# Sample attention of a hybrid decoder: 30 page buffers, operand pairs split two half-steps ahead, and a residual chunk loaded later

## The chip, the cores and the metric

The kernel runs on one core of a Trainium2 chip. The metric is the device time of one execution in microseconds (us). The engines are named as the profile names them: PE is TensorE (PEld its weight loads), DVE is VectorE, ACT is ScalarE, POOL is GpSimd, SP is SyncE, which issues every transfer here.

## What is computed

One inference step of two layers for a prompt of 1024 tokens and for 64 sample tokens (8 sequences of 8). The change is in the attention of the samples, which runs over 2048 cached positions for each sequence, in 16 pages of 128 rows that a table points to:

```
def one(args):
    qn_b, qr_b, c_b, kr_b, pt_b = args
    c_all = concat([ckv_pool[layer, pt_b].reshape(n_past, KV_RANK), c_b])       # 16 pages of 128 x 256
    kr_all = concat([krope_pool[layer, pt_b].reshape(n_past, QK_ROPE_DIM), kr_b])
    k_nope = rms_norm(einsum('bkc,chd->bkhd', c_all, w_uk), g_k_nope)
    s = (q_nope . k_nope + q_rope . kr_all) * SOFTMAX_SCALE
    p = softmax(where(mask, s, -inf))
    lat = einsum('bhqk,bkc->bqhc', p, c_all)          # the cached rows again, now as values
    return einsum('bqhc,chv->bqhv', lat, w_uv)
```

Then attention and pooling outputs go through one output projection, the residual `x` is added, and an MLP follows. All is float32: a matmul operand is split into a high and a low part, and three products stand for one.

## The kernel before, in words

`sample_attention` goes through 8 sequences (called batches, `b`) of 16 pages. One half-step `q` (0 to 15) handles one page of batch `b`: `keys(b, q)` multiplies the transposed page with `w_uk` and the queries (12 matmuls into the banks `pk`), ACT squares the result (`psq`, L990) and copies the scores (L991), and DVE sums the squares by head (`pss`, L992; there is exactly one such instruction to a half-step, so its start times mark the half-steps). At each even `q` the loop also issues the loads of two later pages (`load`, L870 and L871) and transposes the pair after next (`transp`: PE `cpt` L957, ACT `ch` L960, DVE `cl` L961): at step `q` the pages `q+2` and `q+3`.

In the same half-steps the previous batch's softmax and value product run (`slot(b - 1, q)`): exponentials at steps 6 and 7 (`weigh`, ACT L1048 and L1049), their low parts on DVE (`weigh_low`, L1054), and from step 8 to 15 the product of the weights with two cached pages a step (`latent`, PE L1074 and L1075). For that product a page is split once more, this time untransposed: `vsplit` makes the high part `vh` on ACT (L1060) and the low part `vl` on POOL (L1062; partly on DVE in the last batch). `vsplit` is the last reader of a page, so it frees the page's buffer `cp`. There are 26 such buffers; a new page takes the one that came free first.

`norm8(b)` at step 8 takes the reciprocal root of the first 8 pages' sums: two short instructions on DVE (L130, L138) and then 12 on POOL (L141 to L144); `scale8` at step 10 uses it. The order on PE, DVE, ACT and POOL in the loop is that in which the code is written (`manual_schedule`); SP's order is the scheduler's. Each engine works its list in order.

Behind the loop the last batch is drained (`slot` alone), and around this drain `fill` brings in the residual: `residual_load` reads 128 rows of `x` into one of three buffers `raw`, `residual` transposes them on PE (L1246) and ACT copies them into the residual `y` (L1247), which is kept in three chunks of columns (384, 384 and 320 tokens). `mix_load` reads the other inputs of the projection, and `op.chunk(group, c)` is the projection of chunk `c`, whose result DVE adds to `y[c]` (L315). After the drain `w_uv` is read (L1181), its product `so` computed (L1185), and the next weights (`w_out`, L94) are read through the same three buffers.

Of the kernel before, what the change touches and what calls it, by code (L numbers as in the profile page):

```python
# [10 lines left out]
F32 = mybir.dt.float32  # L11
F32R = mybir.dt.float32r
# [8 lines left out]
P = 128  # L21
D = 1024
KB = 8
# [5 lines left out]
CH = [(0, 384), (384, 768), (768, 1088)]  # L29
NTB = 9  # L30
# [5 lines left out]
R = 256  # L36
# [21 lines left out]
def pool(g, name, bufs=1, space=None, side=None):  # L58
    kw = {}
    if space is not None:  # L60
        kw["space"] = space
    if side is not None:
        kw["side"] = side
    if space is not DRAM:
        kw["reuse_waits"] = "tile"
    return g.tc.tile_pool(name=name, bufs=bufs, **kw)
# [771 lines left out]
def sample_attention(g, I, S, ahead, fill_start, fill):  # L838
    nc = g.nc
    SQ = H * DT  # L840
    with ExitStack() as st:
        sa = st.enter_context(pool(g, "sa", 2, side="right"))
# [16 lines left out]
        def load(b, pr):  # L859

            if pr % 2 == 0:
                kps[b, pr // 2] = sk.tile([P, 4, QR], F32, name="kp", tag="kp", bufs=3)
            kp = kps[b, pr // 2]
            for j in range(2):
                pg = pr * 2 + j
                n = b * NPG + pg
                with g.tc.issue_after(dmas[n - 8]) if n >= 8 else nullcontext():
                    v = nc.sync.value_load(ptb[0:1, n:n + 1], min_val=0, max_val=npool - 1)
                cp = sa.tile([P, R], F32, name="cp", tag="cp", bufs=26)
                nc.sync.dma_start(cp, I["cache_ckv"][0, ds(v, 1)].rearrange("o p c -> p (o c)"))  # L870
                di = nc.sync.dma_start(kp[:, (pr % 2) * 2 + j], I["cache_krope"][0, ds(v, 1)].rearrange("o p c -> p (o c)"))  # L871
                dmas.append(di.ins)
                cps[b, pg] = cp
# [44 lines left out]
        fold = sa.tile([P, 2, NS], F32, name="fold", bufs=1)  # L918
        nc.gpsimd.tensor_copy(fold, i2[:, None, :].to_broadcast([P, 2, NS]))

        VT = [(sa.tile([P, R + 2], F32R, name=f"vh{i}", bufs=1), sa.tile([P, R], F32R, name=f"vl{i}", bufs=1)) for i in range(4)]
        for vh, _ in VT:
            nc.gpsimd.memset(vh[:, R:].bitcast(F32), 1.0)
        latT = sa.tile([P, 2, H, NS], F32, name="latT", bufs=1)
# [71 lines left out]
        def norm8(b):  # L996
            ss = ss8[b].rearrange("p a h -> p (a h)")
            r = prs[b] = g.tiny.tile([P, 64], F32, name="prs", tag="prs", bufs=2)
            rsqrt(g, r, ss, 1.0 / QN, 64, eng=nc.gpsimd)

        def scale8(b, g8):
            r = prs.pop(b)
            s8 = sc[b][:, g8 * 8:g8 * 8 + 8]
            sv = s8.rearrange("p a (h t) -> p (a h) t", t=DT)
            nc.vector.tensor_tensor(sv, sv, r.unsqueeze(2).to_broadcast([P, 64, DT]), ALU.mult)
            sf = s8.rearrange("p a q -> p (a q)")
            nc.vector.tensor_tensor(sf, sf, pr8[b].rearrange("p a q -> p (a q)"), ALU.add)
# [8 lines left out]
        def soft1(b):  # L1016
            s = sc[b]
            nc.gpsimd.memset(s[NS:, NPG], NEG)
            nc.gpsimd.tensor_copy(s[:NS, NPG], snew[:NS, b].rearrange("p h t -> p (h t)"))
            mx = mxs[b]  # L1020
            nc.vector.tensor_reduce(mx[:, 1], s[:, 8:].rearrange("p a q -> p q a"), AX.X, ALU.max)
            nc.vector.tensor_tensor(mx[:, 0], mx[:, 0], mx[:, 1], ALU.max)

        def soft2(b):
            pt = msc("mxt")
            nc.tensor.transpose(pt[:SQ, :P], mxs.pop(b)[:, 0], g.ident)
            m1 = g.tiny.tile([P, 1], F32, name="m1", tag="m1", bufs=2)
            nc.vector.tensor_reduce(m1[:SQ], pt[:SQ, :P], AX.X, ALU.max)
            dg = sa.tile([P, SQ], F32, name="sdg", tag="sdg")
            nc.vector.tensor_scalar_mul(dg[:SQ], g.ident[:SQ, :SQ], m1[:SQ])  # L1030
            return dg
# [3 lines left out]
        def soft3(b, dg):  # L1035
            pb = mxb[b] = msc("mxb")
            nc.tensor.matmul(pb[:, :SQ], g.ones[:SQ], dg[:SQ], start=True, stop=True)
            ph_[b] = sa.tile([P, NPG + 1, 2, SQ], F32R, name="ph", tag="ph", bufs=1)
# [17 lines left out]
        vs = {}  # L1056

        def vsplit(b, pg):
            ch, c_l = vs[b, pg] = VT[pg % 4]
            nc.scalar.copy(ch[:, :R], cps[b, pg])  # L1060
            e = nc.vector if b == DB - 1 and pg % 4 else nc.gpsimd
            e.tensor_tensor(c_l, cps.pop((b, pg)), ch[:, :R].bitcast(F32), ALU.subtract)  # L1062
# [41 lines left out]
        def slot(b, q):  # L1104

            if not 0 <= b < DB:
                return
            if q == 0:
                norm8(b)
            elif q == 2:  # L1110
                scale8(b, 1)
            elif q == 3:
                soft1(b)
            elif q == 5:
                st_[b] = soft2(b)
            elif q == 6:
                soft3(b, st_.pop(b))
                shift(b, 0)
                weigh(b, 0)
                shift(b, 1)  # L1120
            elif q == 7:
                weigh_low(b, 0)
                weigh(b, 1)
            elif q == 8:
                weigh_low(b, 1)
            elif q == 16:
                latent(b, NPG)
                lat2(b)
            elif q == 17:
                lat3(b)  # L1130
            elif q == 20:
                lat4(b)
            if 8 <= q <= 15:
                for pg in (2 * q - 16, 2 * q - 15):
                    latent(b, pg)
            if 7 <= q <= 14:
                for pg in (2 * q - 14, 2 * q - 13):
                    vsplit(b, pg)

        begin(0)  # L1140
# [4 lines left out]
        with g.tc.manual_schedule(engines={ET.PE, ET.DVE, ET.Activation, ET.Pool}):  # L1145
            for n in range(2 * NJ):
                b, q = divmod(n, 16)
# [78 lines left out]
def residual_load(g, I, xts, tb):  # L1226
    nc = g.nc
    p = tbp(tb)
    xts[tb] = xt = raw_tile(g)[:, :1024]
    if tb < 8:  # L1230
        nc.sync.dma_start(xt, I["x_prompt"][0, tb * P:(tb + 1) * P, :])
    else:
        nc.sync.dma_start(xt[:p], I["x_sample"].rearrange("b t d -> (b t) d"))


def residual(g, y, xts, tb):

    nc = g.nc
    p = tbp(tb)
    c, off = tb // 3, (tb % 3) * P  # L1240
    xt = xts.pop(tb)
    for hf in range(2):
        pt = bank(g, "up", "xtp2").rearrange("p (a b) -> p a b", b=P)
        for k in range(4):
            kk = hf * 4 + k
            nc.tensor.transpose(pt[:, k, :p], xt[:p, kk * P:(kk + 1) * P], g.ident[:p, :p])  # L1246
        nc.scalar.copy(y[c][:, hf * 4:hf * 4 + 4, off:off + p], pt[:, :, :p])  # L1247
# [237 lines left out]
def step(ctx, tc, I, O):  # L1485
    nc = tc.nc
    g = G()
# [15 lines left out]
    g.ring = {"A": (g.wr, 2)}  # L1503
    constants(g, I)

    def ytiles(p):
        return [p.tile([P, KB, b - a], F32, name=f"y{c}", tag=f"y{c}", bufs=1) for c, (a, b) in enumerate(CH)]


    ya = ctx.enter_context(ExitStack())  # L1510
    g.lo = nc.gpsimd
    with ExitStack() as l0:
        l0p = l0.enter_context(pool(g, "l0", side="right"))
        S.q_s = l0p.tile([P, H, QH], F32, name="q_s")
        S.k_s = l0p.tile([P, H, QH], F32, name="k_s")
        S.kr = l0p.tile([P, NTB, QR], F32, name="kr")
        S.cs_h = l0p.tile([P, R + 2], F32R, name="cs_h")
        S.cs_l = l0p.tile([P, R], F32R, name="cs_l")
        with ExitStack() as a:
            wb = a.enter_context(pool(g, "wb0"))  # L1520
            g.ring["B"] = (wb, 3)
            kept = in_even(g, I, O, S, a)
            gain_columns(g, I)
            g.table = False
            prompt_attention(g, I, S, *kept)
        g.ps = ctx.enter_context(pool(g, "ps5", space=PSUM))
        y, M = [], {}
        op = OutProj(g, I["w_out_even"][0], M, y, "AABBBAAB")

        xts = {}  # L1530

        def ahead(left):
            if left == 24:
                op.load(0)
            elif left == 20:
                op.parts()
            elif left == 8:
                for tb in range(3):
                    residual_load(g, I, xts, tb)

        def fill_start():
            g.x = ctx.enter_context(pool(g, "x"))
            y.extend(ytiles(ya.enter_context(pool(g, "y"))))

        def fill():
            for tb in range(NTB):
                residual(g, y, xts, tb)
                if tb + 3 < NTB:
                    residual_load(g, I, xts, tb + 3)
            g.lo = nc.vector  # L1550
            mix_load(g, S, M, 0)
            op.chunk(0, 0)
            mix_load(g, S, M, 1)
            mix_load(g, S, M, 2)

        so = sample_attention(g, I, S, ahead, fill_start, fill)

    g.lo = nc.vector
    g.tmp = ctx.enter_context(pool(g, "tmp", 2, side="right"))
# [21 lines left out]
    with ExitStack() as a:  # L1581
# [3 lines left out]
        with pool(g, "rp", side="right") as rp:  # L1585
# [11 lines left out]
            y = op.y = ytiles(yp)  # L1597
# [94 lines left out]
```

## Time and profile before

| | us |
|---|---|
| three runs | 2844.66, 2837.19, 2848.45 (median 2844.66) |
| the profiled execution, its own time | 2843.76 |
| its span in the trace | 2842.0 |
| PE busy in the span | 2707.4 (95%) |
| the loop over pages, first to last `pss` | 432.93 to 807.27 |

The span is what the profiler saw between the first and the last instruction; 1.76 us lie around it. PE is busy nearly all of the time, and most of that is in the MLPs, which the change doesn't touch. In the loop over pages the share is lower and the granted clock of PE falls below 1.00 again and again.

### The profile page before, as it was taken

How to read it: one execution, taken by the hardware profiler on the slowest of the kernel's cores; microseconds unless marked ns; L12 is line 12 of the kernel's file. 1: busy time of each engine (PE TensorE's matmuls, PEld its weight loads, DVE VectorE, ACT ScalarE, POOL GpSimd, SP SyncE). 2: the span in 40 equal slices, each digit the busy share in tenths (PEclk: the TensorE clock that was granted, in tenths of full speed). 3: DMA queues.
4: the chain of work that ended last, by engine and by line, in shares of the span. 5: the costliest groups of instructions: out<-in, count | busy, mean ns of one | idle time of the engine just before them, and what ended most of it. 6: DMA issues, size and time to landing. Idle time of an engine off the chain costs nothing.

```text
span 2842.0 us, 42942 instructions
## 1 busy us (share of the span) xinstructions
PE 2707.4 (95%) x16801; PEld 2627.9 (92%) x16801; DVE 1724.3 (61%) x3300; ACT 898.4 (32%) x1878; POOL 425.6 (15%) x627
## 2 busy tenths in 40 slices
PE   6999998888889999999999999998999999999999
PEld 6888888878779999999999998998999999999998
DVE  7666665555554655555555567998365555555555
ACT  5334555555552311111111125665321111111111
POOL 4220002435341100000000023444200000000000
PEclk9999999999989999999999999999999999999999
DMA  4232102212143111111111112113111111111111
GB/s 153 63 115 93 38 24 65 58 39 76 41 120 76 52 45 45 45 45 45 45 45 45 45 52 70 36 48 103 46 51 48 39 50 38 51 38 52 38 38 64
DMA packets 200740, 162.03 MB, mean 57 GB/s; under 512 B 40331, under 2 KB 183148, under 8 KB 199763
## 3 DMA queue, kind: packets, MB, share of 16 engines
q1 hardware_dynamic: 200539, 159.31, 18.6%
q8 instruction: 132, 2.16, 0.3%
q14 instruction: 69, 0.57, 0.1%
HBM read 138.18 MB, written 21.21 MB: 56 GB/s over the span
## 4 chain that ended last, share of the span: by engine, by line
PE 62%; DVE 7%; ACT 1%; issue 0%; DMA 0%; POOL 0%; ACTq 0%; DVEq 0%; POOLq 0%; SPq 0%
PE up L158 26%; PE dn L158 26%; PE op L158 6%; PE pu L158 2%; DVE xl L204 1%; PE pgt L158 1%; DVE v L1411 1%; DVE hs L1442 1%; DVE ig L1426 1%; DVE y L272 0%; DVE t L1427 0%; DVE xl L80 0%; PE pg L158 0%; DVE ig L1435 0%; DVE ta L1429 0%
## 5 line engine op out<-in xcount | busy, mean ns | idle before, releaser
L272 DVE TENSOR_TENSOR y<-y,dn 128x384 f32<-128x384 f32 (+1 forms) x768 | 405.7, 532 | 281.2 <-PE dn L158 278.8
L158 PE MATMUL dn<-hh,whB 128*128 128x384 f32 (+1 forms) x1536 | 506.3, 330 | 3.3 <-DVE y L272 3.1
L158 PE MATMUL dn<-hh,wlB 128*128 128x384 f32 (+1 forms) x1536 | 501.9, 327 | 0.0
L158 PE MATMUL up<-xh,whA 128*128 128x384 f32 (+1 forms) x1536 | 501.7, 327 | 0.0
L158 PE MATMUL up<-xl,whA 128*128 128x384 f32 (+1 forms) x1536 | 501.6, 327 | 0.0
L158 PE MATMUL up<-xh,wlA 128*128 128x384 f32 (+1 forms) x1536 | 501.3, 326 | 0.0
L158 PE MATMUL dn<-hl,whB 128*128 128x384 f32 (+1 forms) x1536 | 500.9, 326 | 0.0
L79 ACT CAST whB<-raw 128x1024 fp32r<-128x1024 f32 (+3 forms) x80 | 79.8, 1034 | 704.0 <-PE dn L158 663.6
L158 PEld LDWEIGHTS dn<-hh,whB 128*128 128x128 f32 x1536 | 288.5, 188 | 11.3 <-DVE y L272 11.2
L158 PEld LDWEIGHTS up<-xl,whA 128*128 128x128 f32 x1536 | 288.5, 188 | 0.4
L158 PEld LDWEIGHTS up<-xh,wlA 128*128 128x128 f32 x1536 | 288.5, 188 | 0.3
L158 PEld LDWEIGHTS up<-xh,whA 128*128 128x128 f32 x1536 | 288.5, 188 | 0.2
L158 PEld LDWEIGHTS dn<-hl,whB 128*128 128x128 f32 x1536 | 288.6, 188 | 0.0
L158 PEld LDWEIGHTS dn<-hh,wlB 128*128 128x128 f32 x1536 | 288.5, 188 | 0.0
L257 DVE SCALAR_TENSOR_TENSOR rl<-up,rs 128x384 f32<-128x384 f32 (+1 forms) x192 | 102.9, 536 | 259.3 <-PE up L158 259.3
L258 ACT ACTIVATE hh<-rl 128x384 fp32r<-128x384 f32 (+1 forms) x192 | 97.0, 505 | 447.7 <-DVE rl L257 447.7
L80 POOL TENSOR_TENSOR wlA<-raw,whA 128x1024 fp32r<-128x1024 f32 (+2 forms) x24 | 57.8, 2413 | 743.7 <-PE dn L158 733.3
L992 DVE TENSOR_REDUCE pss<-psq 128x8 f32<-128x512 f32 x128 | 87.6, 685 | 132.1 <-ACT psq L990 132.0
L158 PE MATMUL pk<-wqh,ch 128*128 128x256 f32 (+1 forms) x512 | 165.6, 323 | 0.0
L158 PE MATMUL pk<-wql,ch 128*128 128x256 f32 (+1 forms) x512 | 158.5, 310 | 0.0
L158 PE MATMUL pk<-wqh,cl 128*128 128x256 f32 (+1 forms) x512 | 158.4, 309 | 0.0
L79 ACT CAST whA<-raw 128x1024 fp32r<-128x1024 f32 (+2 forms) x94 | 98.0, 1044 | 189.8 <-PE up L158 143.5
(562 smaller groups left out, 5326.1 us busy)
## 6 DMA issues: line engine op xcount, KB each, us to landing
raw<-in_w_up_dram SPq DMA_DIRECT2D x64, 512.0 KB
raw<-in_w_down_dram SPq DMA_DIRECT2D x64, 512.0 KB
cp<-in_cache_ckv_dram SPq DMA_DIRECT2D x128, 128.0 KB
raw<-in_w_in_rnn_dram SPq DMA_DIRECT2D x16, 512.0 KB
xt<-in_x_prompt_dram SPq DMA_DIRECT2D x8, 512.0 KB
raw<-in_w_out_even_dram SPq DMA_DIRECT2D x8, 512.0 KB
raw<-in_x_prompt_dram SPq DMA_DIRECT2D x8, 512.0 KB
raw<-in_w_out_rnn_dram SPq DMA_DIRECT2D x8, 512.0 KB
```

The source lines that it names most:

```text
L79: g.nc.scalar.copy(h, src)
L80: (lo or g.nc.vector).tensor_tensor(l, src, h.bitcast(F32), ALU.subtract)
L158: g.nc.tensor.matmul(ps, a, b, start=(i == 0), stop=(i == n - 1))
L204: nc.vector.scalar_tensor_tensor(xl[:, m], yv, gcol[:, m:m + 1], xh[:, m].bitcast(F32), ALU.mult, ALU.subtract)
L257: nc.vector.scalar_tensor_tensor(r[:, :n], ps[:, :n], 0.0, RS[c][:, :n], ALU.max, ALU.mult)
L258: nc.scalar.activation(hh[:, a:b], r[:, :n], AF.Square)
L272: nc.vector.tensor_tensor(y[c][:, m], y[c][:, m], ps[:, :n], ALU.add)
L992: nc.vector.tensor_reduce(ss8[b][:, pg % 8], sq.rearrange("p f (h d) -> p (f h) d", d=QN), AX.X, ALU.add)
L1411: V.scalar_tensor_tensor(v, ul[:, a + k:b + k], vec[:, k, n:n + 1], v, ALU.mult, ALU.add)
L1426: V.scalar_tensor_tensor(t2, t2, 1.0, v, ALU.add, ALU.mult)
L1442: V.tensor_tensor_scan(hs[:, a:b], a0[:, a:b], ig[:, a:b], hs[:, a - 1:a] if a else 0.0, ALU.mult, ALU.add)
```

## The change

The page buffers become 30. The operand pairs `vh`, `vl` become six, and `vsplit` of a page stands one half-step earlier: steps 6 to 13 where it was 7 to 14, so two half-steps ahead of the product that reads it. The third chunk of the residual gets a pool of its own, opened after the drain; its three loads (row blocks 6, 7 and 8) and transposes stand behind the drain and the product with `w_uv` where they stood in `fill`.

```diff
-                cp = sa.tile([P, R], F32, name="cp", tag="cp", bufs=26)
+                cp = sa.tile([P, R], F32, name="cp", tag="cp", bufs=30)
...
-        VT = [(sa.tile([P, R + 2], F32R, name=f"vh{i}", bufs=1), sa.tile([P, R], F32R, name=f"vl{i}", bufs=1)) for i in range(4)]
+        VT = [(sa.tile([P, R + 2], F32R, name=f"vh{i}", bufs=1), sa.tile([P, R], F32R, name=f"vl{i}", bufs=1)) for i in range(6)]
...
-            ch, c_l = vs[b, pg] = VT[pg % 4]
+            ch, c_l = vs[b, pg] = VT[pg % 6]
...
-            if 7 <= q <= 14:
-                for pg in (2 * q - 14, 2 * q - 13):
+            if 6 <= q <= 13:
+                for pg in (2 * q - 12, 2 * q - 11):
                     vsplit(b, pg)
...
-            y.extend(ytiles(ya.enter_context(pool(g, "y"))))
+            y.extend(ytiles(ya.enter_context(pool(g, "y")), (0, 1)))
...
-            for tb in range(NTB):
+            for tb in range(6):
                 residual(g, y, xts, tb)
-                if tb + 3 < NTB:
+                if tb + 3 < 6:
                     residual_load(g, I, xts, tb + 3)
...
         so = sample_attention(g, I, S, ahead, fill_start, fill)
+    y.extend(ytiles(ya.enter_context(pool(g, "y2")), (2,)))
+    for tb in range(6, NTB):
+        residual_load(g, I, xts, tb)
+    for tb in range(6, NTB):
+        residual(g, y, xts, tb)
```

On ACT, at step 6 of a batch, the difference reads (`s` is the score buffer, `ph` the weights' high part; the first two rows are `weigh` of the first 8 pages):

```order
 L1048 ACTIVATE s<-s 128x512
 L1049 CAST ph<-s 128x8x64
+L1060 CAST vh_4919<-cp 128x256
+L1060 CAST vh_4921<-cp 128x256
 L990 ACTIVATE psq<-pk 128x256 x2
 L991 COPY s<-pk 128x64
```

Two page casts now stand between `weigh` and the squares of step 6. At step 7 two casts stand behind the second `weigh` as before, now those of pages 2 and 3.

On POOL, around `norm8` of the second batch, before (the buffer numbers 4919 to 4926 are the four pairs):

```order
L1019 COPY s<-snew 64x64
L1062 TENSOR_TENSOR vl_4920<-cp,vh_4919 128x256
L1062 TENSOR_TENSOR vl_4922<-cp,vh_4921 128x256
L1062 TENSOR_TENSOR vl_4924<-cp,vh_4923 128x256
L1062 TENSOR_TENSOR vl_4926<-cp,vh_4925 128x256
L141 TENSOR_TENSOR rsu<-rsr 128x64
L142 TENSOR_TENSOR rsu<-rsu,rsx 128x64
```

And the same place on POOL now, with six pairs (4919 to 4930):

```order
L1019 COPY s<-snew 64x64
L1062 TENSOR_TENSOR vl_4920<-cp,vh_4919 128x256
L1062 TENSOR_TENSOR vl_4922<-cp,vh_4921 128x256
L1062 TENSOR_TENSOR vl_4924<-cp,vh_4923 128x256
L1062 TENSOR_TENSOR vl_4926<-cp,vh_4925 128x256
L1062 TENSOR_TENSOR vl_4928<-cp,vh_4927 128x256
L1062 TENSOR_TENSOR vl_4930<-cp,vh_4929 128x256
L141 TENSOR_TENSOR rsu<-rsr 128x64
```

Pages 0 to 5 are split ahead of the twelve instructions of `norm8`, where it was pages 0 to 3; behind the twelve, page 6 follows now and page 4 did before.

On SP, the transfers around the drain, before (`raw` is one of the three buffers; `mix_d` and `a_d` are the pooling and attention outputs in DRAM):

```order
L1231 DMA raw<-in_x_prompt_dram 128x1024 x5
L1233 DMA raw<-in_x_sample_dram 64x1024
L1199 DMA raw<-mix_d 128x2x384 x2
L1206 DMA raw<-a_d 128x2x512
...
L1206 DMA raw<-a_d 128x2x512
L1181 DMA raw<-in_w_uv_dram 128x2x512
L1296 DMA vec<-in_conv_w_dram 128x8x1
L94 DMA raw<-in_w_out_even_dram 128x8x128 x2
```

And the same stretch of SP now:

```order
L1231 DMA raw<-in_x_prompt_dram 128x1024 x3
L1199 DMA raw<-mix_d 128x2x384 x2
L1206 DMA raw<-a_d 128x2x512
...
L1206 DMA raw<-a_d 128x2x512
L1181 DMA raw<-in_w_uv_dram 128x2x512
L1296 DMA vec<-in_conv_w_dram 128x8x1
L1231 DMA raw<-in_x_prompt_dram 128x1024 x2
L1296 DMA vec<-in_conv_w_dram 128x8x1 x3
L1233 DMA raw<-in_x_sample_dram 64x1024
L94 DMA raw<-in_w_out_even_dram 128x8x128 x2
```

Three loads of `x` went from ahead of the first `mix_d` to between `w_uv` and the next weights.

## Rows read from the trace of the kernel before

**Rows 1.** The page's first line.

```profile
span 2842.0 us, 42942 instructions
```

**Rows 2.** Waits of PE from 425 to 800 us: in total, times, longest.

```profile
PE cpt L957 <- DMA cp<-in_cache_ckv_dram: 31.8, 14, 4.1
PE lat L1075 <- POOL vl L1062: 16.6, 14, 2.4
```

**Rows 3.** Waits of SP's queue, 400 to 900 us.

```profile
SPq L870 <- POOL vl L1062: 149.7, 31, 16.9
```

**Rows 4.** Timeline of SP: start, duration (us).

```profile
483.59 0.33 SPq L870 DMA_DIRECT2D cp<-in_cache_ckv_dram  x1
```

**Rows 5.** Timeline of DVE: start, duration, in brackets the idle time before and its releaser.

```profile
477.05 0.69 DVE L992 TENSOR_REDUCE pss<-psq 128x8 f32<-128x512 f32 x1
...
483.59 0.69 DVE L992 TENSOR_REDUCE pss<-psq 128x8 f32<-128x512 f32 x1 [1.44 <-ACT psq L990]
488.15 0.69 DVE L961 TENSOR_TENSOR cl<-cpt,ch 128x512 fp32r<-128x512 f32 x1 [3.87 <-ACT ch L960]
488.76 1.09 DVE L1054 TENSOR_TENSOR ph<-s,ph 128x576 fp32r<-128x576 f32 x1
...
490.52 0.20 DVE L138 TENSOR_SCALAR rsr<-rsx 128x64 int32<-128x64 int32 x1
...
503.23 0.69 DVE L992 TENSOR_REDUCE pss<-psq 128x8 f32<-128x512 f32 x1 [1.25 <-ACT psq L990]
...
505.75 0.69 DVE L992 TENSOR_REDUCE pss<-psq 128x8 f32<-128x512 f32 x1 [1.18 <-ACT psq L990]
...
778.47 0.69 DVE L992 TENSOR_REDUCE pss<-psq 128x8 f32<-128x512 f32 x1 [1.43 <-ACT psq L990]
...
797.88 0.69 DVE L992 TENSOR_REDUCE pss<-psq 128x8 f32<-128x512 f32 x1 [0.52 <-ACT psq L990]
```

**Rows 6.** Timeline of ACT.

```profile
479.00 0.63 ACT L1048 ACTIVATE s<-s 128x512 f32<-128x512 f32 x1 [1.35 <-DVE s L1043]
...
482.30 0.70 ACT L1060 CAST vh<-cp 128x256 fp32r<-128x256 f32 x2
```

**Rows 7.** Timeline of POOL: the first row of `norm8`, and the row behind its last.

```profile
490.79 0.29 POOL L141 TENSOR_TENSOR rsu<-rsr 128x64 f32<-128x64 f32 x1 [0.36 <-DVE rsr L138]
...
495.18 3.23 POOL L1062 TENSOR_TENSOR vl<-cp,vh 128x256 fp32r<-128x256 f32 x4
```

**Rows 8.** Timeline of PE, second batch: the second wait for `vl`, and a step's first `pk`.

```profile
497.09 0.39 PE L1075 MATMUL lat<-vl,ph 128*128 128x256 f32 x1 [0.62 <-POOL vl L1062]
...
503.53 0.28 PE L158 MATMUL pk<-wqh,ch 128*128 128x256 f32 x1
```

**Rows 9.** Timeline of PE, third and fifth batch: the first wait for `vl`.

```profile
545.35 0.39 PE L1075 MATMUL lat<-vl,ph 128*128 128x256 f32 x1 [2.36 <-POOL vl L1062]
...
645.24 0.39 PE L1075 MATMUL lat<-vl,ph 128*128 128x256 f32 x1 [1.20 <-POOL vl L1062]
```

**Rows 10.** Windows: length; busy (instructions) by engine; clock granted; DMA share, GB/s.

```profile
545.00:550.00 5.00, 4.03 (x17) 3.78 (x18) 1.53 (x2) 0.41 (x2) 2.80 (x4) 0.58 0.34 88
550.00:555.00 5.00, 5.00 (x33) 4.99 (x33) 2.85 (x4) 3.22 (x11) 1.61 (x3) 0.74 0.34 90
645.00:650.00 5.00, 4.58 (x33) 4.36 (x34) 3.74 (x5) 2.19 (x8) 3.74 (x6) 1.00 0.33 88
```

**Rows 11.** Groups by line on POOL, 415 to 800 us: count, busy us, mean ns.

```profile
L80 POOL TENSOR_TENSOR wlA<-raw,whA 128x1024 fp32r<-128x1024 f32 x2 | 4.7, 2358 | 0.4 <-ACT whA L79 0.4
```

**Rows 12.** Timeline of PE and ACT behind the drain: projection's start, `so`, next weights.

```profile
832.74 1.01 PE L158 MATMUL op<-xh,whA 128*128 128x384 f32 x2 [1.19 <-ACT xh L1200]
...
852.37 2.08 PE L1185 MATMUL so<-raw,latT 128*64 128x64 f32 x32 [0.93 <-DMA raw<-in_w_uv_dram]
...
865.77 0.34 PE L158 MATMUL op<-xh,whB 128*128 128x384 f32 x1
...
858.33 1.05 ACT L79 CAST whB<-raw 128x1024 fp32r<-128x1024 f32 x1 [1.07 <-DMA raw<-in_w_out_even_dram]
```

More of the change, by code (lines that the diff above doesn't have):

```diff
@@ L1504, in step, with ytiles @@
     constants(g, I)
-    def ytiles(p):
-        return [p.tile([P, KB, b - a], F32, name=f"y{c}", tag=f"y{c}", bufs=1) for c, (a, b) in enumerate(CH)]
+    def ytiles(p, cs=(0, 1, 2)):
+        return [p.tile([P, KB, b - a], F32, name=f"y{c}", tag=f"y{c}", bufs=1) for c, (a, b) in enumerate(CH) if c in cs]
     ya = ctx.enter_context(ExitStack())
```

## The prediction

> **What bounds the kernel now.** I read PE's share first: it is busy nearly always, so only a stretch in which it isn't can give time back without a matmul less. Then the waits of PE in the loop over pages: it loses 31.8 us to page loads, in 14 waits, and 16.6 us to `vl`, in 14 waits [rows 2]. Two waits of each kind fall into each batch but the first, so these are two places in a batch, not noise. Then SP's own waits, for the reason why loads are late: its page loads waited 149.7 us for `vl` on POOL [rows 3], the last reader of a page, so for a free buffer. In the second batch the load goes out at 483.59 [rows 4], just behind step 7, whose `pss` starts at 483.59 too [rows 5]: the count agrees. At step 8 PE transposes pages 10 and 11, so 12 pages of this batch must be in, and with 26 buffers two pages of the batch before must have been split by then; their split stands at step 7.
>
> What the two waits cost is read from the pace of `pss`. From step 7 to step 11 it takes 503.23 - 483.59 = 19.64 us in the second batch and 797.88 - 778.47 = 19.41 in the eighth [rows 5]; over these seven batches 19.64, 20.76, 19.53, 17.55, 18.72, 19.73 and 19.41, mean 19.33. An undisturbed step with value products takes 505.75 - 503.23 = 2.52 [rows 5], so four would be 10.1. Some 9 us a batch are lost, 65 in all, which is more than the waits themselves (48.4): the rest is clock. After the wait of 2.36 us at 545.35 [rows 9] the window from 545 has a granted clock of 0.58 and the next 0.74 [rows 10], a mixture of the two levels 1.2 and 2.4 GHz.
>
> **The page loads.** With 30 buffers 14 pages of a batch fit beside all 16 of the one before, so the transposes up to step 10 need nothing freed, and steps 12 and 14 need what is now split from step 6 on. The load wait goes away. Its cover is the lead of the buffers: a load that starts when the buffer comes free has four half-steps.
>
> **The earlier split.** It puts two casts, 0.70 us [rows 6], in front of the squares of step 6 and keeps two in front of those of step 7. ACT is the limit there: it starts `weigh` at 479.00, and from then every row follows on the one before, up to the squares of step 7. So `pss` of step 7 comes 0.70 later. The two pairs more are two memsets on POOL long before the loop's end and cost nothing.
>
> **What is late next.** Here I leave the plain account, in which the 65 us come back. POOL's list has `norm8`, and PE now meets the pages behind it. The chain for one batch, from the start of `pss` at step 7:
> - DVE goes on to `cl` 0.64 later (it had to wait 4.56 for the load: 488.15 - 483.59), and from `cl` to the first POOL row of `norm8` it took 490.79 - 488.15 = 2.64 [rows 5, 7]. Together 3.28.
> - `norm8` holds POOL for 495.18 - 490.79 = 4.39 [rows 7]: 7.67.
> - Then POOL splits two pages. PE could start on the second `vl` at 497.09 [rows 8], 1.91 after POOL began: 9.58. These were pages 4 and 5 for step 10; now they are pages 6 and 7 for step 11.
> - The last product takes 0.22, and from a step's first `pk` (503.53) to its `pss` (505.75) it is 2.22 [rows 5, 8]: step 11 has its `pss` 12.02 after step 7.
>
> PE would be at step 11 earlier: between the `pss` of 7 and page 6 it has the rest of steps 8 to 10, three steps of 2.52, so 7.6, less what it is ahead of ACT at step 7; I take 1.6 for that, an estimate (ACT's rows from 479.00 to 483.59 [rows 5, 6] are 4.6 us for what PE does in two steps less the value products). It arrives at about 6, against 8.45 for the first `vl` (7.67 and 0.78 for one split). So it waits some 2.4 us and then 0.6 more, as at 545.35 and 497.09. The wait for `vl` isn't removed by the lead of two half-steps; it moves one step on. What is gained is that the chain starts 3.9 us sooner.
>
> **The clock after that wait.** After 2.36 us the windows lost (1 - 0.58) x 5 + (1 - 0.74) x 5 = 3.4 us of full speed, the wait itself within; after 1.20 us the window from 645 stayed at 1.00 [rows 9, 10]. So 0 to 3.4; I take 1.6, about the middle, since 2.4 is like the first but a part of its loss was the wait. The Trainium skill ("TensorE: Matmul & The Clock Gate", Why this matters for your kernels) asks for matmul bursts without long idle gaps, and a gap as short as this is within what it allows; by it the term would be 0. The row at 545 disagrees, so the row's side is taken, and the page's case is a rival below.
>
> **The sum of the loop.** 19.33 - 0.70 - 12.02 - 1.6 = 5.0 us a batch, 35 in seven. In the sixth batch two weight splits, 4.7 us [rows 11], stand on POOL ahead of its `norm8`. Before, they hid behind the load wait; now they lengthen the chain by up to that. I take 4 off: 31.
>
> **Behind the drain.** Bounded from both sides. Gain: the projection starts at 832.74 with 1.19 us of idle time before it, PE waits 0.93 for `w_uv` [rows 12], and with three loads fewer ahead of `mix_d` both may go; two vl pairs more are ready when the last products begin, some 0.8. With a slow clock around these waits I set 4.6 as the end. Loss: the three loads now stand between `w_uv` and the next weights, which are cast at 858.33 and used at 865.77 [rows 12]. The second cast ends 1.05 later and its low part another 1.2, so there are some 5 us to spare, and the queue gets there three loads sooner; only the load of block 8 waits for something new, the buffer of `so`. If all three loads came on top at some 2.4 us each and the waits were as long again, the loss would be 7. I take a gain of 2, nearer to nothing than to the end. The transposes of the chunk are only moved.
>
> **Sum.** 31 + 2 = 33 us from the profiled 2843.76 (its span of 2842.0 [rows 1] and 1.76 around it) gives 2811. The median of the runs, 2844.66, is 0.9 above that execution, so no correction is made. Something below 0.5% (14 us) can't be told from no change here, since three runs spread over 11 us.
>
> **Rivals.**
> 1. The plain account: PE runs free past step 7. The first to last interval would be PE's arrival of 6, 0.3 for the products, and 2.22, so 8.5; 19.33 - 0.70 - 8.5 = 10.1 a batch, 71, with the drain 73: 2771. Against it: `norm8` stands where it stands on POOL and takes 4.39 [rows 7]. For it: nothing in the rows but the chance that DVE reaches `norm8` far sooner.
> 2. The clock stays up after the moved wait: the term of 1.6 is 0, the loop gives 46 - 4, and the time is 2800. For it, the wait of 1.20 with 1.00; against it, that of 2.36.
> 3. POOL is late for `norm8`: two more splits are queued ahead of it. If DVE is ready first, `norm8` waits for up to both, 1.91 a batch [rows 7, 8], 13 in all: 2824. The 1.09 us of `weigh_low` (488.76) beside POOL's splits [rows 5] speaks for some slowing. The Trainium skill ("SBUF — State Buffer", SBUF: two separate sides) says that GpSimd and a DVE instruction with two SBUF inputs exclude each other at a shared port. By it these splits and `weigh_low`, which now come together in each batch, would run one after the other, which is this rival again.
> 4. The loads stay late, because SP's list is in order and something else in it waits (the three small buffers `kp`, or the loads of `x`). Then only the casts count, 0.70 x 7 = 5, less 2 behind the drain: 2847. Against it: the row for `cp` names POOL's `vl` for 149.7 us [rows 3].
> 5. Slower: the moved wait keeps PE at 1.2 GHz. Each us at that level costs half a us of matmuls; the loop's gain without a clock term is 6.6 a batch, so it decides from 13.2 us a batch at 1.2 GHz, longer than all the steps from 11 to the next batch (five of 2.52). With all of the remaining half at 1.2 GHz and the softmax steps too, some 22 us, the loss is 11 - 6.6 = 4.4 a batch, 31 in all: 2873. Rows 10 speak against it: in the second window the clock is on its way back.
>
> **Chances.** Forecast 0.57; rivals: 1, 0.08; 2, 0.16; 3, 0.11; 4, 0.05; 5, 0.03. The forecast's own bounds are a clock term up to 3.4 (13 us later) and a drain that loses 7 (9 later), or gains 4.6 and a sixth batch for nothing (7 sooner): singly 2804 to 2824. The range 2790 to 2828 takes in rivals 2 and 3 and leaves out 1, 4 and 5, 0.16 together, and some mishaps of the rest. Faster by over 0.5%: forecast, 1, 2 and nearly all of 3, 0.89; the same: 4 and a little of 3, 0.08; slower: 0.03.
>
> **What would show it.** Right: no wait of PE for `cp` in the loop; SP's wait for `vl` gone or without effect; two waits of PE for `vl` in each of seven batches, now at step 11 and behind `norm8`; `pss` from step 5 to 7 longer by 0.7; from 7 to 11 some 13.6. Wrong: a wait for `cp` that stays (rival 4), no wait for `vl` (rival 1), or an idle PE between 855 and 870 in the old count for the block 8 or the weights.

## The result, and the profile after

The changed kernel takes 2806.67 us (median of 4 runs, 2805.04 to 2809.78), the kernel before 2843.05 (with one run more than was shown ahead). The ratio is 0.9874, 95% interval 0.9852 to 0.9896: 36 us faster. The forecast was 2811, the range 2790 to 2828.

The profiled execution after took 2805.04 us with a span of 2803.3 and a mean clock of 0.987 (before: 2842.0 [rows 1], 0.977). The waits of PE in the loop over pages, 425 to 775 us, and SP's wait for free page buffers in the same stretch (total, times, longest):

```profile
PE lat L1075 <- POOL vl L1062: 22.2, 16, 3.0
PE lat L1074 <- DVE ph L1054: 5.9, 7, 0.9
PE cpt L957 <- DVE cl L961: 4.2, 1, 4.2
PE kpt L969 <- PE pk L158: 3.9, 7, 0.6
...
SPq L870 <- POOL vl L1062: 77.5, 23, 9.5
```

The wait of `cpt` for the load, 31.8 us in [rows 2], is gone. The wait for `vl` has grown from 16.6 to 22.2: it took over a part of what the other gave up. The wait for `ph` (`weigh_low`, at step 8) is new, and that of `cpt` for `cl` stands in the first batch, before as after. SP still waits for buffers, half as long as in [rows 3], and no longer holds up PE. The chain in the second batch, first on DVE, from `pss` of step 7 (484.04) to that of step 11 (496.90), where [rows 5] had 483.59 and 503.23:

```profile
484.04 0.69 DVE L992 TENSOR_REDUCE pss<-psq 128x8 f32<-128x512 f32 x1 [1.44 <-ACT psq L990]
484.65 0.68 DVE L961 TENSOR_TENSOR cl<-cpt,ch 128x512 fp32r<-128x512 f32 x1
...
487.03 0.20 DVE L138 TENSOR_SCALAR rsr<-rsx 128x64 int32<-128x64 int32 x1
...
491.77 1.20 DVE L1005 TENSOR_TENSOR s<-s,prs 128x512 f32<-128x512 f32 x1 [2.42 <-POOL prs L144]
...
496.90 0.69 DVE L992 TENSOR_REDUCE pss<-psq 128x8 f32<-128x512 f32 x1 [1.65 <-ACT psq L990]
```

Then on POOL (the pair of pages 4 and 5, the first and last row of `norm8`, the splits behind it), and on PE, from the first product of step 8 and then at step 11:

```profile
484.99 1.95 POOL L1062 TENSOR_TENSOR vl<-cp,vh 128x256 fp32r<-128x256 f32 x2 [0.31 <-ACT vh L1060]
487.30 0.29 POOL L141 TENSOR_TENSOR rsu<-rsr 128x64 f32<-128x64 f32 x1 [0.36 <-DVE rsr L138]
...
491.42 0.32 POOL L144 TENSOR_TENSOR prs<-rsu,rsr 128x64 f32<-128x64 f32 x1
491.69 4.63 POOL L1062 TENSOR_TENSOR vl<-cp,vh 128x256 fp32r<-128x256 f32 x6
```

```profile
482.76 0.36 PE L1074 MATMUL lat<-vh,ph 128*128 128x258 f32 x1 [0.84 <-DVE ph L1054]
...
489.94 0.36 PE L1074 MATMUL lat<-vh,ph 128*128 128x258 f32 x1
492.47 0.39 PE L1075 MATMUL lat<-vl,ph 128*128 128x256 f32 x1 [2.17 <-POOL vl L1062]
493.61 0.38 PE L1075 MATMUL lat<-vl,ph 128*128 128x256 f32 x1 [0.63 <-POOL vl L1062]
```

`cl` no longer waits for a load (0.61 after `pss`, where it was 4.56), and everything behind it comes sooner by that; PE is done with the first product of step 11 at 490.30 (489.94 + 0.36) and waits 2.17 and 0.63 for two pages that stand behind `norm8`. The granted clock behind this wait, in the second and then in the third batch (windows; columns as in rows 10; 1.00 is 2.4 GHz, a value between 0.50 and 1.00 a mixture with 1.2 GHz):

```profile
489.00:494.00 5.00, 2.21 (x15) 1.79 (x14) 2.54 (x4) 1.88 (x7) 4.42 (x11) 1.00 0.16 46
494.00:499.00 5.00, 5.00 (x29) 4.96 (x29) 2.63 (x4) 2.26 (x7) 3.02 (x5) 0.66 0.41 96
...
532.00:537.00 5.00, 2.58 (x19) 2.17 (x17) 2.54 (x4) 2.65 (x9) 4.26 (x12) 1.00 0.12 30
537.00:542.00 5.00, 4.63 (x36) 4.60 (x36) 3.38 (x5) 2.49 (x8) 4.31 (x7) 1.00 0.38 92
```

The same wait (2.17 in both) was followed by 0.66 in one and by 1.00 in the other. The sixth batch has the two weight splits on POOL ahead of pages 4 and 5 and of `norm8`, and PE waits at steps 10 and 11, POOL first and then PE:

```profile
658.70 5.23 POOL L80 TENSOR_TENSOR wlA<-raw,whA 128x1024 fp32r<-128x1024 f32 x2 [0.48 <-ACT whA L79]
663.90 1.41 POOL L1062 TENSOR_TENSOR vl<-cp,vh 128x256 fp32r<-128x256 f32 x2
```

```profile
664.66 0.39 PE L1075 MATMUL lat<-vl,ph 128*128 128x256 f32 x1 [3.00 <-POOL vl L1062]
...
670.44 0.39 PE L1075 MATMUL lat<-vl,ph 128*128 128x256 f32 x1 [1.49 <-POOL vl L1062]
671.58 0.39 PE L1075 MATMUL lat<-vl,ph 128*128 128x256 f32 x1 [0.63 <-POOL vl L1062]
```

The pace of `pss`, read from the starts of its 128 rows on DVE in each profiled execution (us; "loop" is from the first `pss` to the last, the others are means over the last seven batches, and "6th" is the interval 7 to 11 of the sixth batch). All kernels of the next section are in it:

```
kernel                          loop   5->7   7->11   11->15   6th
before                         374.3   6.55   19.33    9.84   18.72
after                          338.1   7.16   13.39   10.00   17.67
e1 residual alone              377.8   6.55   19.82    9.84   20.26
e2 e1 + 30 buffers             345.2   6.55   15.16    9.85   18.12
e3 e1 + early split            339.0   7.16   13.77    9.72   17.44
e4 after, low 6, 7 on DVE      314.2   7.16   11.98    7.98   15.83
e5 e4 with 26 buffers          321.9   7.16   12.90    8.16   15.87
e6 after, norm8 on DVE         316.5   7.17   12.60    7.56   16.22
e7 after, weights later        333.9   7.16   12.77   10.00   11.99
e8 e6 + e7                     310.8   7.17   11.98    7.57   11.91
e9 e8 with 26 buffers          323.9   7.17   12.81    8.39   13.07
e10 e4 + e7                    311.1   7.17   11.31    8.00   11.28
```

So the loop gave 36.2 us (374.3 - 338.1), and what lies behind it 2.4 (2842.0 - 807.3 against 2803.3 - 771.0, single executions; more on this below).

### The profile page after: what moved, and what is told of

Same layout as the page of the kernel before. It is cut to its first block, busy times and chain, and to the rows that moved or that the text cites. A ratio compares the mean times of both kernels' runs of the same rounds, so it can differ in the third digit from the quotient of the medians.

```text
span 2803.3 us, 42991 instructions
## 1 busy us (share of the span) xinstructions
PE 2685.6 (96%) x16801; PEld 2608.5 (93%) x16801; DVE 1727.3 (62%) x3300; ACT 895.9 (32%) x1878; POOL 425.2 (15%) x629
## 4 chain that ended last, share of the span: by engine, by line
PE 62%; DVE 8%; ACT 1%; issue 0%; DMA 0%; POOL 0%; ACTq 0%; DVEq 0%; SPq 0%; POOLq 0%
PE up L158 27%; PE dn L158 26%; PE op L158 5%; PE pu L158 2%; DVE xl L204 1%; DVE v L1411 1%; DVE ig L1426 1%; DVE hs L1442 1%; PE pgt L158 1%; DVE ta L1429 0%; DVE t L1427 0%; DVE xl L80 0%; DVE y L272 0%; DVE ig L1435 0%; PE otp L1628 0%
## 5 line engine op out<-in xcount | busy, mean ns | idle before, releaser
L259 DVE TENSOR_TENSOR rl<-rl 128x384 f32<-128x384 f32 (+1 forms) x192 | 106.1, 552 | 77.7 <-ACT hh L258 77.4
```

The lines of the kernel that those rows point to most:

```text
L259: nc.vector.tensor_tensor(r[:, :n], r[:, :n], r[:, :n], ALU.mult)
```

## Experiments

The theory: the load wait goes through the buffers, the wait for `vl` stays because of `norm8` on POOL, and this chain (`pss` 7, `cl`, `norm8`, pages 6 and 7) now sets the pace. Rivals: one part of the change makes all of the gain; the splits or DVE are the limit, not `norm8`; the work behind the loop matters more than thought.

**The parts of the change.** Three kernels start from the one before. e1 has only the residual's edit; e2 adds the first line below, e3 the other three edits. Both contain e1's, which frees in SBUF (10 KB a partition) what the buffers and the pairs take (4 and 4.1).

```diff
-                cp = sa.tile([P, R], F32, name="cp", tag="cp", bufs=26)
+                cp = sa.tile([P, R], F32, name="cp", tag="cp", bufs=30)
...
-VT = [... for i in range(4)]
+VT = [... for i in range(6)]
-            ch, c_l = vs[b, pg] = VT[pg % 4]
+            ch, c_l = vs[b, pg] = VT[pg % 6]
-            if 7 <= q <= 14:
-                for pg in (2 * q - 14, 2 * q - 13):
+            if 6 <= q <= 13:
+                for pg in (2 * q - 12, 2 * q - 11):
```

> The kernel before with only the residual's third chunk moved (26 page buffers, four pairs, split from step 7 on, as before). The theory that the gain lies in the loop and that the drain gives about 2 us (the bounds of the prediction were -7 and +4.6) expects 2841, a loop that is not shorter by more than 1 us between its first and last pss, and the mix load and the w_uv load sooner behind the loop. A rival, that the shorter queue behind the loop is a real part of the 36 us, expects 2830 or less. A second one, that the moved loads come on top, expects 2850.

2842.88 us, ratio 0.9995 (0.9986 to 1.0004): no difference that can be told. Its loop is 3.4 us longer in this execution, though nothing in the loop is changed; after a wait of 1.62 us at step 10 of the sixth batch the clock from 690 to 710 is 0.91, after the same wait of 1.64 before it was 1.00 (windows, before and then e1):

```profile
690.00:710.00 20.00, 17.73 (x132) 16.78 (x131) 10.73 (x16) 12.18 (x40) 11.00 (x19) 1.00 0.31 87
...
690.00:710.00 20.00, 17.66 (x119) 16.73 (x119) 9.77 (x14) 10.93 (x36) 10.98 (x19) 0.91 0.32 86
```

That is how far single executions differ.

> The kernel before with the residual moved and 30 page buffers, but four operand pairs, split from step 7 on. The load wait needs only the buffers, so it is gone here. But the pages behind norm8 on POOL are still pages 4 and 5, which PE wants at step 10: they are there 9.6 us after the pss of step 7, step 10 has its pss 12.0 after it and step 11 another 2.5 later, 14.5, with 1.6 to 3 for a clock that drops after a longer wait of some 5 us: 16 to 17.5 against 19.3 before. That is 2 to 3 us a batch, 13 to 23 in seven, and with 2 of the drain 2818 to 2828. Rival, the buffers alone are all of the change: 2807. Rival, the wait for vl takes up all that the load wait gave: 2841.

2816.32 us, ratio 0.9901 (0.9887 to 0.9915): 28 us, a little more than forecast. The wait for `cp` is gone, the one for `vl` grew, and in the second batch PE waits at step 10 where `norm8` starts at 484.78. Waits of PE (425 to 775 us), then its timeline:

```profile
PE lat L1075 <- POOL vl L1062: 22.2, 30, 2.7
PE lat L1074 <- ACT vh L1060: 4.9, 7, 0.7
```

```profile
489.94 0.39 PE L1075 MATMUL lat<-vl,ph 128*128 128x256 f32 x1 [2.66 <-POOL vl L1062]
491.08 0.39 PE L1075 MATMUL lat<-vl,ph 128*128 128x256 f32 x1 [0.63 <-POOL vl L1062]
```

From `pss` 7 to 11 the one ordinary batch with a clock of 1.00 throughout, the second, took 14.2 (14.5 expected). Two with a slower clock behind the wait took 15.7 and 16.9. In the other three the slower clock falls into steps 8 and 9, ahead of the wait, which is then shorter (1.09 in the third batch), and they took 13.7 to 13.8. Window of the third batch, whose `pss` 7 is at 525.54:

```profile
526.00:531.00 5.00, 4.82 (x24) 4.62 (x24) 3.35 (x6) 2.19 (x8) 3.93 (x9) 0.66 0.48 118
```

The first wait in the second batch was 2.66 and not 5: PE was at step 10 at 487.28, 5.75 after `pss` 7, where I had worked with 3.5. Some 1.4 of that were waits for `vh` and `vl` at step 8 that I had not counted.

> The kernel before with the residual moved, six operand pairs and the split from step 6 on, but 26 page buffers. Two pages are now freed a step sooner, so the load that PE waits for goes out some 2 to 2.5 us sooner; the wait for cp becomes shorter by about that and does not vanish (31.8 us before; some 10 to 16 now). The chain over cl and norm8 starts later than with 30 buffers by what is left of that wait, so step 11 has its pss 13.5 to 14.5 us after step 7, with the clock 15 to 17, and step 7 comes 0.7 later: a gain of 1.6 to 3.6 a batch, 11 to 25 in seven, and with the drain 2817 to 2831. Rival, the earlier split alone is all of the change: 2807. Rival, without buffers it gives nothing: 2841.

2805.67 us, ratio 0.9863 (0.9849 to 0.9877): as fast as the whole change. My expectation was wrong and the first rival right. The loads are late as I expected (PE's waits, 425 to 775 us):

```profile
PE cpt L957 <- DMA cp<-in_cache_ckv_dram: 18.5, 14, 2.0
PE lat L1075 <- POOL vl L1062: 8.3, 9, 2.9
```

but the time is no longer. In the second batch (PE, then DVE's `pss` of step 7 and `cl`, then POOL's first row of `norm8` and the splits behind it):

```profile
482.69 0.44 PE L957 MATMUL cpt<-ident,cp 128*128 128x128 f32 x2 [1.88 <-DMA cp<-in_cache_ckv_dram]
483.86 0.69 PE L957 MATMUL cpt<-ident,cp 128*128 128x128 f32 x2 [0.73 <-DMA cp<-in_cache_ckv_dram]
...
494.20 0.39 PE L1075 MATMUL lat<-vl,ph 128*128 128x256 f32 x1 [0.63 <-POOL vl L1062]
```

```profile
483.39 0.69 DVE L992 TENSOR_REDUCE pss<-psq 128x8 f32<-128x512 f32 x1 [1.44 <-ACT psq L990]
485.21 0.69 DVE L961 TENSOR_TENSOR cl<-cpt,ch 128x512 fp32r<-128x512 f32 x1 [1.13 <-ACT ch L960]
```

```profile
487.87 0.29 POOL L141 TENSOR_TENSOR rsu<-rsr 128x64 f32<-128x64 f32 x1 [0.36 <-DVE rsr L138]
...
492.27 4.66 POOL L1062 TENSOR_TENSOR vl<-cp,vh 128x256 fp32r<-128x256 f32 x6
```

PE idles 1.88 + 0.73 at step 8 in place of 2.17 at step 11, beside the chain over POOL, which ends last either way. The chain starts 1.2 later (`cl` 1.82 after `pss` 7, not 0.61), and 7 to 11 takes 13.0 to 13.2 in most batches, 12.0 + 1.2. But the slower clock, where there is one, now falls into steps 8 to 10, where PE would wait for POOL anyway. Windows of the third batch:

```profile
528.00:533.00 5.00, 5.00 (x28) 4.92 (x27) 3.23 (x5) 2.52 (x8) 3.42 (x7) 0.66 0.43 118
533.00:538.00 5.00, 4.45 (x35) 4.23 (x34) 3.58 (x5) 3.66 (x12) 4.50 (x10) 1.00 0.11 29
```

In the changed kernel it falls behind step 11, where nothing covers it. From 7 to 15 the two kernels take 23.49 and 23.39 in the mean. So the load wait isn't free: with the clock at 1.00 throughout, 7 to 15 takes 22.66 here (the fourth batch) against 21.70 in the changed kernel, 1.0 more. But a slower clock adds only 0.1 to 0.5 here, and 1.56 in four of six batches there. Nothing ties these two amounts together: that the kernels come out level is chance. I had added the clock on top of the chain instead of asking where it lies.

**The chain over POOL.** e4 takes two low parts off it:

```diff
-            e = nc.vector if b == DB - 1 and pg % 4 else nc.gpsimd
+            e = nc.vector if pg in (6, 7) or b == DB - 1 and pg % 4 else nc.gpsimd
```

> The changed kernel with the low parts of pages 6 and 7 made on DVE in every batch and not on POOL. If what PE waits for at step 11 is norm8 ahead of these two splits on POOL, the two waits (22.2 us in all) go, and most of the clock's drops behind them (about 1 us in five of seven batches): from pss of step 7 to that of step 11 it takes 9 to 10 and not 12.7, and the time falls by 18 to 26 us, to 2781 to 2789. Rival, the wait moves on to pages 8 and 9, which stand behind norm8 now, as it moved from step 10 to step 11: 2800 to 2807. Rival, the two subtractions on DVE delay the chain of cl, pss and scale8 there by as much as they save: 2807 or later.

2782.51 us, ratio 0.9787 (0.9774 to 0.9800): 24 us less than the changed kernel. The wait for `vl` is 6.9 us (8 waits), 3.2 of it in the sixth batch, and the ordinary batches take 18.9 to 19.6 from 7 to 15, so none has a drop of 1.5. But 7 to 11 took 11.3 in five of them, not 9 to 10, and 11 to 15 took 8.0 in place of 10.0: at step 10 DVE waits for POOL with the reduction of `pss` queued behind, while PE runs on.

```profile
529.97 1.21 DVE L1005 TENSOR_TENSOR s<-s,prs 128x512 f32<-128x512 f32 x1 [2.04 <-POOL prs L144]
```

So `pss` is a marker of PE's pace only where DVE isn't late itself; 7 to 15 as one piece (20.0 against 23.4) tells the gain. The same kernel with 26 buffers:

> As e4 (low parts of pages 6 and 7 on DVE, residual moved, six pairs, split from step 6 on), but with 26 page buffers. The theory after e2 and e3: the load wait and the chain over norm8 lie beside each other, and each covers the other; 30 buffers are worth nothing while POOL is late at step 11, and something once it is not. Then the load waits of e3 (18.5 us in 14 waits, 1.9 and 0.7 in a batch) have nothing behind them any more and come on top of e4's 2782.5 with a little clock: 2798 to 2807. Rival, the earlier split alone makes the loads early enough and the rest hides: 2783, as e4.

2790.24 us, ratio 0.9811 (0.9797 to 0.9826): the buffers are worth 7.7 us here, half or less of what I expected. The load wait is back in full, and only a part of it costs. Waits of PE, 425 to 775 us, and DVE in the fourth batch:

```profile
PE cpt L957 <- DMA cp<-in_cache_ckv_dram: 18.6, 14, 2.1
```

```profile
574.47 1.21 DVE L1005 TENSOR_TENSOR s<-s,prs 128x512 f32<-128x512 f32 x1 [1.54 <-POOL prs L144]
```

DVE still waits for `prs`; what shows in the pace is the lateness of that chain, 12.90 - 11.98 = 0.9 a batch from 7 to 11 and 0.2 from 11 to 15 (9.17 in the second batch, the others as in e4), 7.7 in seven, and not PE's 2.7 of waiting.

**norm8 on DVE, the weight split, and both.** e6 has `eng=None` in place of `eng=nc.gpsimd` in `norm8`; e7 has `elif left == 17:` in place of `elif left == 20:` ahead of `op.parts()`; e8 both.

> The changed kernel with norm8's Newton steps on DVE (nine small instructions there in place of twelve on POOL, whose span is 4.4 us). If it is norm8 that makes vl late at step 11, those waits go as in e4, and DVE need not wait for prs before scale8 (2 us idle in e4 at that place), so pss runs evenly from step 7 on: about 10 us from 7 to 11, PE's waits for vl under 8 us in the loop, the sixth batch's included, and the time 2777 to 2786. Rival, POOL's splits themselves are too slow, norm8 or not: the waits stay above 15 us and the time is 2797 or more. Rival, DVE is now late for cl and the reductions, and PE waits for these: 2790 or more.

2782.16 us, ratio 0.9783 (0.9768 to 0.9797), as e4. The waits for `vl` fall to 3.2 us, both in the sixth batch. So it is `norm8` and not the splits themselves. The last rival has a part too: from 7 to 11 most batches take 11.9, not the 10 expected, and PE waits 11.7 us for `cl` (8 waits). 4.1 of that is the wait of the first batch, which the changed kernel has too; the other 7.6 is one wait in each of seven batches at step 10, because DVE is held by `norm8` now. One batch of it (DVE, then PE):

```profile
528.50 0.69 DVE L147 TENSOR_TENSOR rsu<-rsr 128x64 f32<-128x64 f32 x1
529.22 0.23 DVE L148 SCALAR_TENSOR_TENSOR rsu<-rsu,rsx 128x64 f32<-128x64 f32 x1
...
530.00 0.65 DVE L148 SCALAR_TENSOR_TENSOR rsu<-rsu,rsx 128x64 f32<-128x64 f32 x1
...
531.89 0.23 DVE L149 SCALAR_TENSOR_TENSOR prs<-rsu,rsr 128x64 f32<-128x64 f32 x1
```

```profile
533.96 0.66 PE L957 MATMUL cpt<-ident,cp 128*128 128x128 f32 x4 [0.93 <-DVE cl L961]
```

> The changed kernel with the weight split of the sixth batch (two casts on ACT, 4.0 us, and two subtractions on POOL, 5.2 us) three steps of the pages' loop later by its count, so that it stands at step 14 of the batch and not at step 8, ahead of norm8. In the changed kernel this batch takes 17.7 us from pss 7 to pss 11 where the others take 12.7. If POOL's subtractions ahead of norm8 are what costs it 5 us, it takes 12.7 too, the loop is 4 to 5 us shorter, and the time 2800 to 2804. Rival, ACT's 4.0 us cost the same wherever they stand, because PE runs out of pk buffers: the 5 us move to steps 14 and 15 and the time stays at 2806 to 2808.

2804.38 us, ratio 0.9859 (0.9842 to 0.9876). The time alone can't tell this from the changed kernel, the trace can: the sixth batch takes 11.99 from 7 to 11 and 9.71 from 11 to 15, so the casts cost nothing at the new place, and the loop is 4.2 us shorter. The profiled time shows none of it (2804.84 against 2805.04): what lies behind the loop took 4.9 longer in this execution (2803.0 - 765.8 against 2803.3 - 771.0), most of it in layers that the change doesn't touch. With `norm8` or its two splits off POOL the same edit takes 6.2 us (e8 against e6) and 3.8 (e10 against e4) from the medians.

> e6 and e7 together, a try at a version that beats both kernels. If both theories hold, the gain of e6 and most of the 5 us of e7: 2773 to 2782. Rival, once norm8 is not on POOL the weight split's place does not matter: the same as e6.

2775.91 us, ratio 0.9764 (0.9749 to 0.9778): both gains hold, 31 us less than the changed kernel. Two last kernels: e8 with 26 buffers, and e4 with e7's change.

> e8 (norm8 on DVE, weight split later) with 26 page buffers instead of 30. In e5 the load waits came back at their full 18.6 us but cost only 7.7, because POOL's norm8 still held DVE at scale8 (pss from 7 to 11: 12.3 against 11.3). If it is that chain which hides them, then here, with norm8 on DVE, every us by which cl is late moves the whole chain: cl comes 1.2 to 1.8 us later in seven batches, so 8 to 13 us, some clock with it: 2784 to 2791. Rival, DVE's longer norm8 covers the loads even better than POOL's did: 2776 to 2780. Rival, the full wait shows: 2794 or more.

2787.28 us, ratio 0.9800 (0.9780 to 0.9820): 11.4 us for the buffers, as expected. From 7 to 11 it takes 12.81 against 11.98, and from 11 to 15 8.39 against 7.57, this in the three batches in which it took 9.2 to 9.7; these are the three in which the granted clock falls behind `pss` 7 (0.71 from 525 to 530, 0.66 from 568 to 573, 0.74 from 733 to 738).

> e4 with the weight split at step 14 of the batch (e7's change). The sixth batch took 15.8 us from pss 7 to pss 11 in e4 where the others took 11.3, so 4.5 should go: 2776 to 2780, level with e8 (2776). Rival, with less idle time on PE the weight split's casts on ACT now cost at their new place: 2781 to 2783.

2778.68 us, ratio 0.9772 (0.9752 to 0.9793), level with e8; the sixth batch is like the others (11.28). Two ways of taking PE's path off POOL end at the same time, within the noise.

## Why the prediction was right

**The page loads**: right in the row (no wait of PE for `cp`), but not in what it is worth. The working gives the 30 buffers the whole 3.9 us by which the chain starts sooner, because `cl` waits for the load. `cl` came 3.95 sooner (4.56 to 0.61), but e3 has 2.74 of that from the earlier split alone (4.56 to 1.82), which also puts pages 4 and 5 ahead of `norm8`. The buffers add the last 1.2, and beside the split the time shows nothing of it, since a slower clock then falls where it costs more. Without the split the buffers give 27 us (e2 against e1), and once POOL is out of the way 8 to 11 (e5, e9). Each part removes the same lateness from one chain: 27 and 37 us beyond e1 singly (2842.88 less 2816.32 and 2805.67), 36 together.

**The earlier split**: 0.70 forecast, 7.16 - 6.55 = 0.61 measured.

**What is late next**: right, and closely. The forecast put the two waits at step 11 at 2.4 and 0.6; they are 2.17 and 0.63. PE was to arrive at about 6 and did at 6.26 (490.30 - 484.04), in part by luck: both numbers behind it were too large, three steps of 7.6 for 7.18 (482.76 to 489.94) and a lead of 1.6 for 1.28 (484.04 - 482.76), and they were subtracted. From 7 to 11 it was 12.02 without the clock; the third and the last batch, without a drop, took 11.99. e4 and e6 show the cause by taking it away in two ways. One term in it was a little off: a step with value products isn't 2.52 when undisturbed but takes 2.6 or 2.2 on PE (in e4's third batch the first product of steps 9, 10 and 11 starts at 523.22, 525.83 and 528.01), as the page transposes stand in it or not.

**The clock**: the term of 1.6 in every batch was too large; a drop costs that much, but not each batch has one. From 7 to 15 a batch without a drop takes 11.99 + 9.71 = 21.70, one with a drop 12.86 + 10.40 = 23.26, so 1.56 where 1.6 was set. That these agree is luck, since 1.6 was the middle between nothing and 3.4; and it came in four of the six ordinary batches. It is also spread past step 11, so that 7 to 11 took 12.68 in these six and not 13.6. With that the six batches gained 6.15 each (19.44 - 12.68 - 0.61) where 5.0 was forecast. Four drops are 6.2 us where six times 1.6, 9.6, were taken off: this is most of what put the forecast too late.

**The sixth batch**: it is 5.0 longer from 7 to 11 than the others, where 4 was taken off, and e7 shows that the weight split's place is the cause (the two splits hold POOL for 5.23 at 658.70, not 4.7). It gained only 0.4.

**The sum of the loop**: 6 x 6.15 + 0.4, less 1.1 for 11 to 15 (10.00 against 9.84), is 36.2; the forecast was 31.

**Behind the drain**: a gain of 2 was taken. By the first `hh` of the layers behind, the profile shows 4.1 (951.1 - 807.3 = 143.8 before, 910.7 - 771.0 = 139.7 after), of which the unchanged code behind gave 1.7 back. That code took 1890.9 to 1896.9 us over the twelve executions, so 2 us can't be told there, and e1's time shows none. e1, which has this part of the change alone, shows 1.9 by the same `hh` (951.9 - 810.0 = 141.9). The term's sign is likely and its size stays open. The rows of `hh` before and after (ACT, 760 to 1500 us; first and last start), then a window of the changed kernel:

```profile
L258 ACT ACTIVATE hh<-rl x73: 463/524/527, 951.1 to 1497.6; 128x384 fp32r<-128x384 f32 x49, 128x320 fp32r<-128x320 f32 x24
...
L258 ACT ACTIVATE hh<-rl x77: 463/524/527, 910.7 to 1496.9; 128x384 fp32r<-128x384 f32 x52, 128x320 fp32r<-128x320 f32 x25
...
811.00:831.00 20.00, 20.00 (x154) 19.34 (x153) 8.81 (x29) 6.46 (x12) 1.95 (x2) 1.00 0.69 151
```

The two waits that the working named, 1.19 ahead of the projection and 0.93 for `w_uv`, are gone. PE is busy through this window and the 20 us behind it, which take in 855 to 870 of the old count (36.3 earlier now), so the sign of a loss didn't come; two waits of 0.5, at 806.59 and 809.10, are new.

**The rivals**: 1 falls with the waits at step 11; its time of 2771 is not reached even without them (2776 to 2783), since DVE is the next to be late. 2 holds in two batches of six. 3 did not come in the ordinary batches: POOL is done with pages 4 and 5 at 486.94 and idle for 0.36 when `norm8` is ready, though this pair took 1.95 beside `weigh_low`, 0.5 more than the others. 4 and 5 fall with the rows.

## What to carry to other kernels

Where two waits lie beside each other, the sum of their rows tells neither's worth: follow the chain that ends last, and ask for every part of a change what it would give with the others already made. A few microseconds of small work on an engine matter by what is queued behind them in order; moving the queued work or the small work to another engine gave 24 us here, beside the 36 of the buffers and the new split order. A lost clock has a place too: it cost 1.56 us where nothing else ended later, and 0.1 to 0.5 where the chain over POOL did.

## What the hardware showed

The clock after a wait isn't settled by the wait's length: e1 and the kernel before differ after the same wait, and in the changed kernel 2.17 us was followed by 0.66 in the second batch and by 1.00 in the third, and e2's 2.66 by 1.00 (window 490 to 495), but its 2.67 and 2.65 in the fifth and eighth batch by 0.74 and 0.50 (623 to 628, 760 to 765). What decides it stays open. The Trainium skill ("TensorE: Matmul & The Clock Gate", Why this matters for your kernels) allows gaps as short as these; four of the six ordinary batches here disagree.

In e6 a small DVE instruction (L147 to L149) takes 0.65 to 0.69 us while POOL splits pages (its rows: four pages at 525.75 in 3.35 us, two at 529.77 in 1.48) and 0.22 or 0.23 between and after. In the changed kernel POOL's pairs take 1.95 beside `weigh_low` (484.99) and 1.42 to 1.44 alone. So `norm8` on DVE is 5.1 us long at step 8 (527.03 to 532.12), and 2.7 at step 0 (505.62 to 508.36), where POOL is idle. The Trainium skill ("SBUF — State Buffer", SBUF: two separate sides) says that GpSimd and a DVE instruction with two SBUF inputs lock each other out at a shared port. The rows agree: beside the splits the DVE instruction lasts about as long as one split (1.43 for two).
